# Neighbourhood attention with the value products of two heads side by side on column halves of the array, the bias row loaded ahead, and vector work spread over the feed-forward blocks

## The chip, the cores and the metric

One core of one Trainium2 chip runs the whole program. The metric is device time in microseconds (us), the median of the runs. Names of engines in the profile: PE is the matrix engine (TensorE), PEld its weight loads, DVE is VectorE, ACT is ScalarE, POOL is GpSimd, SP is SyncE, which issues nearly all DMAs.

## The reference, cut to what matters

Two blocks of two layers each work on 512 tokens of width 1024 (in the first block with 256 context tokens). Only three parts of the first block bear on the change: the neighbourhood attention of layer 0, the modulation vectors, and the feed-forward of both layers.

```
# layer 0: 16 heads of width 64, latent tokens on an 8 x 64 grid
s_loc = q_row . k_win + bias          # a window of 8 rows x 16 columns around each query
s_ctx = q_row . k_c                   # and all 256 context keys
p = softmax(concat(s_loc, s_ctx))
o = p[..., :n_loc] . v_win + p[..., n_loc:] . v_c
# context queries attend to the 256 context keys only; then out = o @ w_o
ada_mod = split(silu(cvec) @ ada_w[i] + ada_b[i], 6)      # shift, scale, gate vectors
ffn = (silu(h @ w_in_a) * (h @ w_in_u)) @ w_out
```

## The kernel before, in words

The program runs in phases: layer 0 mixer (to about 557 us), layer 0 feed-forward (to about 1190), layer 1 mixer, layer 1 feed-forward (1690 to 2075), then the second block. Weight products split both operands into a rounded high part and a rest and take three products (`mm3`, L146 to L148), each at one column a cycle.

**Attention (`na_heads`, L656 on).** A cell is one head `h` and one block `b` of 128 queries: 16 heads times 6 blocks (b 0 to 3 are latent and see 256 window keys and 256 context keys, b 4 and 5 are context and see 256). 96 cells run head by head, in a loop of steps `g`. Step `g` issues, in this order: the scores of cell g+1 (`na_scores`, PE, into `s`), the store of cell g-3 (`na_store`, DVE), the transposes of cell g-1's probabilities (`na_turn`, PE, `p` to `pt`), the maximum of cell g+1 (DVE), its exponential (ACT, which writes `p` and the sum into a column of `mx`), the value products of cell g-2 (`na_values`, PE), the copy of `pt` to `pT` (ACT for odd b, DVE for even b), and the reciprocal of the sum (`na_scale`, DVE). PE and DVE keep this order as written (`manual_schedule`); the other engines and the DMAs are put in order by the scheduler. Between these pieces `upto` issues units of the query, key and value projections (`pacc`, `ptq`), spread over the first 75 steps, and after them the units of `gemv_rows`. So the stage has a main stretch (about 75 to 412 us) and a tail (about 412 to 512 us) in which only the vector work is left to put between the cells.

The value product of a cell is `pT` (128 keys by 128 queries) as the stationary operand and 64 columns of `v` as the moving one, in plain float32: 4 products for a latent cell, 2 for a context cell, each of two instructions in the trace. The result has queries on partitions; `na_store` multiplies it by the reciprocal. `split_rows` (from step 84 on, one head pair each) transposes it with PE into `pacc` and splits it into `hT`, the operand of the output projection (`pw`).

**Modulation vectors.** `gemv_rows` (layer 0) works in 16 chunks of 256 columns: per chunk two `half` units load 512 KB (`araw`) and issue four products each on four column groups of 32 (`pg`, two result rows per group); ACT copies `pg` to `modx`, a DMA writes the bias row into row 2 of `modx`, and `total` (L475) adds the groups and the bias with one product. Five chunks run in the main stretch, eleven in the tail.
In the feed-forward blocks `gemv_jobs` computes 24 chunks for later layers on DVE (L430, L432: eight multiply-adds of 128x256 for each vector). After each of the 22 inner blocks `f`, `every` = 2 jobs are issued until none are left, so they sit behind f = 0 to 11; `gemv_flush` adds each result on PE behind the next block.

Of the kernel before, what the change touches and what calls it, by code (L numbers as in the profile page):

```python
# [9 lines left out]
F32 = mybir.dt.float32  # L10
# [5 lines left out]
OP = mybir.AluOpType  # L16
# [33 lines left out]
def fr(ap):  # L50
    return ap.bitcast(F32)
# [233 lines left out]
def ffn(S, l, xs, xout, more):  # L285
# [11 lines left out]
    fp, ps = S.tp, S.ps  # L297
    gts = []
    jobs = [j for wn, ll, p, vv in more for j in gemv_jobs(S, fp, wn, ll, p, vv, ps, ("gv", 1))]
    every = (len(jobs) + 18) // 19  # L300
    late = (1000, 300)[l]

    def dense(f):
# [19 lines left out]
    for gi, gn in enumerate(groups):  # L323
        gts = []
        for f in range(f0, f0 + gn):
            pa, pu, *pc = dense(f)
            out_mm = S.lastmm
            g = fp.tile([128, n], F32, name="g", tag="g", bufs=2)
            sa = fp.tile([128, n], F32, name="sa", tag="sa", bufs=2)
            nc.scalar.activation(sa[:, 0:512], pa, AF.Silu)  # L330
            if l == 0:
                gv = g[:, 0:512].rearrange("p (r c) -> p c r", r=ROWS)
                nc.vector.tensor_mul(gv, *[x.rearrange("p (c r) -> p c r", r=ROWS) for x in (sa[:, 0:512], pu)])
            else:
                nc.vector.tensor_mul(g[:, 0:512], sa[:, 0:512], pu)
            if nt == 6:
                nc.scalar.activation(sa[:, 512:768], pc[0][:, 0:256], AF.Silu)
                nc.vector.tensor_mul(g[:, 512:768], sa[:, 512:768], pc[0][:, 256:512])
            gh = fp.tile([128, n], F32R, name="gh", tag="gh", bufs=7)
            gl = fp.tile([128, n], F32R, name="gl", tag="gl", bufs=7)  # L340
            nc.scalar.activation(gh, g, AF.Copy)  # L341
            nc.vector.tensor_sub(gl, g, fr(gh))
            gts.append((gh, gl))
            gemv_flush(S, fp, ps, ("gv", 1), out_mm.ins)
            S.late = late
            for j in jobs[:every]:
                jobs.pop(0)()
        if ys is None:
            ys = [xout(t) for t in range(nt)]
            gates = [gate_bcast(S, "g2", l, v) for v in range(2 if nt == 6 else 1)]  # L350
        last = gi == len(groups) - 1
        Ws = []

        def out_tile(i, h):
            S.mark("ffn_out")
            p = ps.tile([128, 512], F32, name="po", tag="out", bufs=2)
            sl = slice(i * 128, (i + 1) * 128)
            for k in range(gn):
                S.mm3(p, [q[:, sl] for q in gts[k]], Ws[h](k), k == 0, k == gn - 1)
            residual_add(S, ys[i], p, gates[i // 4], h * 512, 512)  # L360

        cols = lambda h: S.weights([S.wcols(wo, h * 512, 512, f0, gn)], gn)
        if last:
            Ws += [cols(0), cols(1)]
            for i in range(nt):
                for h in range(2):
                    out_tile(i, h)
        else:
            for h in range(2):
                Ws.append(cols(h))  # L370
                for i in range(nt):
                    out_tile(i, h)
        f0 += gn
# [69 lines left out]
def gemv_rows(S, wname, layer, parts):  # L443

    nc, ps = S.nc, S.ps
    w = S.I[wname][layer]
    bias = S.I[{"ada_w": "ada_b", "w_ada_2": "b_ada_2"}[wname]]  # L450
    pg = ps.tile([128, 512], F32, name="pg", tag="gv", bufs=1)
    nc.vector.memset(pg[:, 0:256], 0.0)
    sel = S.sb.tile([128, 2], F32, name="sel4")
    nc.vector.tensor_reduce(sel, S.idf.rearrange("p (j v) -> p v j", j=4)[:, 0:2, :], axis=AX.X, op=OP.add)
    nc.vector.tensor_add(sel, sel, S.idf[:, 2:3].to_broadcast([128, 2]))
    todo = []

    def half(part, c, h):
        S.mark(f"gemv {part}{layer}")
        c0 = PARTS[wname].index(part) * D + c * 256  # L460
        raw = S.gvpool.tile([128, 4, 256], F32, name="araw", tag="araw", bufs=2)
        nc.sync.dma_start(raw, S.wcols(w, c0, 256, 4 * h, 4))
        for k in range(4):
            nc.tensor.matmul(pg[32 * k:32 * k + 2, 0:256], S.cc[:, 4 * h + k, :], raw[:, k, :], start=(h == 0),
                             stop=(h == 1))
        if h:
            x = S.gvpool.tile([128, 256], F32, name="modx", tag="modx", bufs=1)
            nc.scalar.activation(x, pg[:, 0:256], AF.Copy)
            nc.sync.dma_start(x[2:3, :], bias[layer:layer + 1, c0:c0 + 256])
            todo.append((part, c, x))  # L470

    def total():
        part, c, x = todo.pop(0)
        S.mark(f"gemv {part}{layer}")
        nc.tensor.matmul(pg[0:2, 256:512], sel, x, start=True, stop=True)  # L475
# [12 lines left out]
    out[-1].append((0.5, total))  # L488
    return out

# [167 lines left out]
def na_heads(S, na, hT, jobs):  # L658
# [11 lines left out]
    S.oT = oT = [S.x4(name="oT") for _ in range(6)]  # L670

    both = na.tile([128, 768], F32, name="bias")
    nc.gpsimd.memset(both[:, 256:512], 0.0)
    S.bias = [(both[:, o:o + 256], view(both, o, ([step, 2], [1, 256]))) for o, step in ((0, 256), (512, -256))]
    QK, V = {}, {}
# [30 lines left out]
            units.pop(0)[1]()  # L706


    cells = [(h, b) for h in range(16) for b in range(6)]
    st = {}  # L710
    fill(NA_HEAD)
    with S.tc.manual_schedule(engines=NA_ENG):
# [8 lines left out]
        for g in range(-1, 100):  # L721
# [3 lines left out]
            if cell(g + 1):  # L725
                h, b = cells[g + 1]
                assert S.nturn[h // 2] == 12, (g, h)
                if b == 0:
                    wide = na.tile([128, 384], F32, name="wide", tag="wide", bufs=2)
                    nc.sync.dma_start(wide, I["rpb_w"][h])  # L730
                    st["wide"] = wide
                st[g + 1] = {}
                na_scores(S, na, st, g + 1, h, b, QK[h // 2][h % 2], mask)
            if cell(g - 3):
                na_store(S, st.pop(g - 3), *cells[g - 3], oT)
            upto(g + NA_S[0])
            if cell(g - 1):
# [3 lines left out]
            upto(g + NA_S[1])  # L741
            if cell(g + 1):
                na_exp(S, st[g + 1], *cells[g + 1])
            if cell(g - 2):
                h = cells[g - 2][0]
                assert cells[g - 2][1] or len(V[h // 4][1]) == 3, g
                na_values(S, st[g - 2], *cells[g - 2], V[h // 4])
            if cell(g - 1):
                na_copy(S, st[g - 1], *cells[g - 1])
            if 84 <= g < 91:  # L750
# [183 lines left out]
                F.then(NA_LAGS[5] + NA_GAP * (2 * u + hh), lambda a=(tt, u, hh): turn(*a), 0.2)  # L934


def split_rows(S, oR, oT, pr):

    nc = S.nc
    S.mark("osplit")  # L940
    for ts, (hi, lo) in ((range(4), oR.row(pr)), (range(4, 6), oR.crow(pr))):
        pt = S.acc(128 * len(ts))
        for i, t in enumerate(ts):
            nc.tensor.transpose(pt[:, i * 128:(i + 1) * 128], oT[t][:, pr * 128:(pr + 1) * 128], S.idf)
        nc.scalar.activation(hi, pt, AF.Copy)
        nc.vector.tensor_sub(lo, pt, fr(hi))


def na_scores(S, na, st, g, h, b, qk, mask):
# [16 lines left out]
    me.update(s=s, p=S.t2("p", n), mx=sb.tile([128, 4], F32, name="mx", tag="mx", bufs=7))  # L966
    if lat:
        if b == 0 or BVAR[b] != BVAR[b - 1]:
            S.bias.reverse()
            o = BOFF[b] * 8  # L970
            nc.gpsimd.tensor_sub(S.bias[0][0], mask[:, BVAR[b], :], st["wide"][:, o:o + 256])
        me["bias"] = S.bias[0][1]


def na_max(S, me, h, b):
# [14 lines left out]

def na_scale(S, me):
    S.mark("attscale")
    r = me["mx"][:, 3:4]
    S.nc.vector.reciprocal(r, r)


def na_turn(S, me, h, b):
# [17 lines left out]
        nc.vector.tensor_copy(pT, pt)  # L1015


def na_values(S, me, h, b, V):
    nc = S.nc
    S.mark(f"att{h}.{b}")  # L1020
    vc = (h % 4) * 64
    vt, vs = V
    vv = vt[4:6]
    if b < 4:
        k0 = KBASE[b] * 8
        vv = [vt[k0 // 128 + j] if k0 % 128 == 0 else vs[k0 // 128 + j] for j in range(2)] + vv
    po = S.ps.tile([128, 64], F32, name="po", tag="pv", bufs=1)
    for j, v in enumerate(vv):
        nc.tensor.matmul(po, me["pT"][:, j, :], v[:, vc:vc + 64], start=(j == 0), stop=(j == len(vv) - 1))
    me["po"] = po  # L1030
# [754 lines left out]
```

## Time and profile before

| | us |
|---|---|
| median of 3 runs | 3476.13 (3475.0 to 3479.37) |
| the profiled execution: its own time | 3472.26 |
| its span, first to last instruction | 3470.5 |
| mean granted PE clock | 0.984 of full speed |

The profiled execution is the one from which every row below is taken. Its own time is 3.87 us under the median of the runs. PE is busy for 97% of the span, but a busy PE is not PE at its peak: the record of a short product lasts longer than the distance to the next one, so prices are read below from start to start.

### The profile page before, as it was taken

The page shows a single profiled execution, that of the slowest core. Times are in us where ns is not written, and L with a number is a line of the kernel's source. Part 1 is how long each engine was busy: PE and PEld are TensorE (multiplying, and loading weights), DVE is VectorE, ACT ScalarE, POOL GpSimd, SP SyncE. Part 2 cuts the span into 40 slices and gives each one's busy share as a digit, 9 for nine tenths or more (in the row PEclk, how much of TensorE's full clock was granted, in tenths as well). Part 3 has the DMA queues.
Part 4 walks back from the last instruction along what each step waited for, and adds up shares of the span by engine and source line. Part 5 has one row for each costly group of instructions (what it writes and reads, how often), then busy time and mean ns, then how long its engine had stood idle before and what let it go on. Part 6 is the DMA issues. An engine that isn't in the chain of part 4 may idle for free.

```text
span 3470.5 us, 49643 instructions
## 1 busy us (share of the span) xinstructions
PE 3355.7 (97%) x18924; PEld 2838.8 (82%) x18924; DVE 1892.7 (55%) x3745; ACT 1259.4 (36%) x2480; POOL 720.1 (21%) x650
## 2 busy tenths in 40 slices
PE   7999989999999999999999999999999999999999
PEld 5999857887788788888777878888888788888887
DVE  6456544649864556578778544435552334355523
ACT  4455533222222433334422334333333343333332
POOL 2122202111111211101322223121222221211222
PEclk9999989999999999999999999999999999999999
DMA  6122244324531121111556434232223432322333
GB/s 202 49 75 67 63 135 141 97 67 128 176 116 56 54 62 44 55 49 49 163 165 195 119 108 125 80 104 73 92 78 101 144 104 80 110 69 91 94 97 100
DMA packets 450206, 345.30 MB, mean 99 GB/s; under 512 B 40336, under 2 KB 421552, under 8 KB 449968
## 3 DMA queue, kind: packets, MB, share of 16 engines
q1 hardware_dynamic: 449536, 341.73, 32.9%
q8 instruction: 148, 2.42, 0.3%
q0 software_dynamic: 432, 0.41, 0.1%
q14 instruction: 90, 0.74, 0.1%
HBM read 328.34 MB, written 12.74 MB: 98 GB/s over the span
## 4 chain that ended last, share of the span: by engine, by line
PE 74%; DVE 7%; DMA 2%; ACT 2%; issue 1%; POOL 1%; DVEq 0%; SPq 0%; POOLq 0%; ACTq 0%
PE pacc L148 12%; PE pacc L147 12%; PE pacc L146 12%; PE pau L148 3%; PE pau L146 3%; PE pau L147 3%; PE po L146 3%; PE po L148 3%; PE po L147 3%; PE pw L148 2%; PE pw L146 2%; PE pw L147 2%; DVE gacc L432 2%; PE pl L1194 2%; DVE wlo L135 1%
## 5 line engine op out<-in xcount | busy, mean ns | idle before, releaser
L135 POOL TENSOR_TENSOR wlo<-wraw,whi 128x512 fp32r<-128x512 f32 x388 | 526.7, 1359 | 2121.9 <-ACT whi L132 1762.1
L132 ACT ACTIVATE whi<-wraw 128x512 fp32r<-128x512 f32 x776 | 485.2, 631 | 796.9 <-PE pacc L147 357.8
L135 DVE TENSOR_TENSOR wlo<-wraw,whi 128x512 fp32r<-128x512 f32 x388 | 332.1, 857 | 552.1 <-ACT whi L132 547.4
L148 PE MATMUL pacc<-hT,wlo 128*128 128x512 f32 x1344 | 535.1, 398 | 0.0
L146 PE MATMUL pacc<-hT,whi 128*128 128x512 f32 x1344 | 534.6, 398 | 0.0
L147 PE MATMUL pacc<-hT,whi 128*128 128x512 f32 x1344 | 532.0, 396 | 0.0
L146 PE MATMUL pacc<-whi,hT 128*128 128x256 f32 x1056 | 307.4, 291 | 5.0 <-DVE h L607 2.9
L148 PEld LDWEIGHTS pacc<-hT,wlo 128*128 128x128 f32 x1344 | 252.8, 188 | 58.3
L147 PEld LDWEIGHTS pacc<-hT,whi 128*128 128x128 f32 x1344 | 252.7, 188 | 57.7
L147 PE MATMUL pacc<-wlo,hT 128*128 128x256 f32 x1056 | 299.4, 284 | 0.2 <-DVE wlo L813 0.2
L148 PE MATMUL pacc<-whi,hT 128*128 128x256 f32 x1056 | 298.4, 283 | 0.0
L146 PEld LDWEIGHTS pacc<-hT,whi 128*128 128x128 f32 x1344 | 253.0, 188 | 54.7
L146 PE MATMUL pau<-hT,whi 128*128 128x512 f32 x704 | 280.0, 398 | 0.7 <-DVE h L607 0.7
L148 PE MATMUL pau<-hT,wlo 128*128 128x512 f32 x704 | 280.2, 398 | 0.0
L147 PE MATMUL pau<-hT,whi 128*128 128x512 f32 x704 | 279.1, 396 | 0.0
L432 DVE SCALAR_TENSOR_TENSOR gacc<-araw,cact,gacc 128x256 f32<-128x256 f32 x392 | 222.0, 566 | 23.8 <-DMA araw<-ada_w 10.6
L146 PEld LDWEIGHTS pacc<-whi,hT 128*128 128x128 f32 x1056 | 200.5, 190 | 7.7 <-DVE h L607 3.1
L147 PEld LDWEIGHTS pacc<-wlo,hT 128*128 128x128 f32 x1056 | 200.9, 190 | 2.0 <-DVE wlo L813 0.4
L148 PEld LDWEIGHTS pacc<-whi,hT 128*128 128x128 f32 x1056 | 200.4, 190 | 0.0
L146 PE MATMUL po<-whi,gh 128*128 128x512 f32 x440 | 177.7, 405 | 17.0 <-ACT gh L341 15.7
L147 PE MATMUL po<-wlo,gh 128*128 128x512 f32 x440 | 175.6, 400 | 0.0
L148 PE MATMUL po<-whi,gl 128*128 128x512 f32 x440 | 175.1, 400 | 0.1
(375 smaller groups left out, 6600.4 us busy)
## 6 DMA issues: line engine op xcount, KB each, us to landing
araw<-ada_w SPq DMA_DIRECT2D x96, 512.0 KB
wraw<-w_in SPq DMA_DIRECT2D x96, 512.0 KB
wraw<-ffn_w_in SPq DMA_DIRECT2D x176, 256.0 KB
wraw<-w_in SPq DMA_DIRECT2D x160, 256.0 KB
araw<-w_ada SPq DMA_DIRECT2D x48, 512.0 KB
wraw<-ffn_w_out SPq DMA_DIRECT2D x40, 512.0 KB
x<-x SPq DMA_DIRECT2D x24, 512.0 KB
wraw<-hg_w_in SPq DMA_DIRECT2D x24, 512.0 KB
```

The lines of the kernel that those rows point to most:

```text
L132: nc.scalar.activation(hi, r, AF.Copy)
L135: eng.tensor_sub(lo, r, fr(hi))
L146: nc.tensor.matmul(out, lh[0], rh[0], start=first, stop=False)
L147: nc.tensor.matmul(out, lh[0], rh[1], start=False, stop=False)
L148: self.lastmm = nc.tensor.matmul(out, lh[1], rh[0], start=False, stop=last)
L432: nc.vector.scalar_tensor_tensor(acc, r, cv, acc, op0=OP.mult, op1=OP.add)
L1194: nc.tensor.matmul(pl[:, c, :], KX[:, c * 128:(c + 1) * 128], view(Q, c * 128, ([2 * m, 64 // m], [LAT + m, 2], [1, m])), start=True, stop ...
```

## The change

It does four things.
1. **Value products.** The 96 cells run in pairs of heads: (2p, b), (2p+1, b). In every odd step the products of both cells of a pair are issued together: now 64 columns of `v` are stationary and `pT` moves (128 columns), the first head goes to output partitions 0 to 63 and the second to 64 to 127, that is to one half of the array's columns each. The result has the head's channels on partitions, so the four transposes in `split_rows` are gone, and one copy per pair replaces two stores. As queries no longer stand on partitions there, DVE scales `p` by the reciprocal before the transposes (`na_scale`). The bias tiles belong to the parity of the head, and the `wide` tiles of a pair are loaded at its start.
2. **Bias row apart.** Its DMA goes to row 98 of `modx`, which ACT doesn't write, and is issued at the chunk's first half instead of behind the ACT copy.
3. **Vectors spread.** The 24 jobs of a feed-forward block go to f = 0 to 19 in proportion: two behind f = 0, 5, 10 and 15, one behind each other one.
4. **By itself**: `split_rows` no longer takes two `pacc` banks, which the output projection uses.

```diff
@@ ffn
-    every = (len(jobs) + 18) // 19
+    njobs = len(jobs)
-            for j in jobs[:every]:
+            while jobs and (njobs - len(jobs)) * 20 < njobs * (f + 1):
                 jobs.pop(0)()
@@ gemv_rows
+    m = 3 * 32 + 2
+        if h == 0:
+            x = S.gvpool.tile([128, 256], F32, name="modx", tag="modx", bufs=1)
+            nc.sync.dma_start(x[m:m + 1, :], bias[layer:layer + 1, c0:c0 + 256])
+            todo.append((part, c, x))
         if h:
-            x = S.gvpool.tile([128, 256], F32, name="modx", tag="modx", bufs=1)
-            nc.scalar.activation(x, pg[:, 0:256], AF.Copy)
-            nc.sync.dma_start(x[2:3, :], bias[layer:layer + 1, c0:c0 + 256])
-            todo.append((part, c, x))
+            nc.scalar.activation(todo[0][2][0:m, :], pg[0:m, 0:256], AF.Copy)
@@ na_heads
-    cells = [(h, b) for h in range(16) for b in range(6)]
+    cells = [(2 * pr + i, b) for pr in range(8) for b in range(6) for i in range(2)]
-            if cell(g - 3):
+            if cell(g - 3) and g % 2 == 0:
-            if cell(g - 2):
+            if cell(g - 2) and g % 2:
-                na_values(S, st[g - 2], *cells[g - 2], V[h // 4])
+                na_values(S, [st[g - 3], st[g - 2]], *cells[g - 2], V[h // 4])
@@ split_rows
-        pt = S.acc(128 * len(ts))
-        for i, t in enumerate(ts):
-            nc.tensor.transpose(pt[:, i * 128:(i + 1) * 128], oT[t][:, pr * 128:(pr + 1) * 128], S.idf)
-        nc.scalar.activation(hi, pt, AF.Copy)
-        nc.vector.tensor_sub(lo, pt, fr(hi))
+        nc.scalar.activation(hi, o_row(oT, pr, lat), AF.Copy)
+        nc.vector.tensor_sub(lo, o_row(oT, pr, lat), fr(hi))
@@ na_scale
     S.nc.vector.reciprocal(r, r)
+    S.nc.vector.tensor_scalar(p, p, r, None, op0=OP.mult)
@@ na_values
-    po = S.ps.tile([128, 64], F32, name="po", tag="pv", bufs=1)
+    po = S.ps.tile([128, 128], F32, name="po", tag="pv", bufs=1)
     for j, v in enumerate(vv):
-        nc.tensor.matmul(po, me["pT"][:, j, :], v[:, vc:vc + 64], start=(j == 0), stop=(j == len(vv) - 1))
+        for i, me in enumerate(two):
+            nc.tensor.matmul(po[64 * i:64 * i + 64, :], v[:, vc + 64 * i:vc + 64 * i + 64], me["pT"][:, j, :],
+                             start=(j == 0), stop=(j == len(vv) - 1))
@@ na_store
-    S.nc.vector.tensor_scalar(oT[b][:, h * 64:(h + 1) * 64], me["po"], me["mx"][:, 3:4], None, op0=OP.mult)
+    S.nc.vector.tensor_copy(o_row(oT, h // 2, b < 4)[:, (b % 4) * 128:(b % 4 + 1) * 128], me["po"])
```

The new line numbers are some lines higher. Three places show how the order moves.

DVE in the main stretch, before: one step and the start of the next (`s,mx` is the maximum, `cat` and `qn` belong to the projections).

```order
L1015 COPY pT<-pt 128x256
L994 RECIPROCAL mx<-mx 128x1
L1036 TENSOR_SCALAR oT<-po,mx 128x64
L477 COPY modb<-pg 2x256
L884 TENSOR_TENSOR qn<-pacc,gain 128x2x128 x2
L981 ISA s,mx<-s,bias 128x512
```

The same place after the change: the scaling of `p` follows each reciprocal, and the store is a copy that comes once in two steps.

```order
L1023 COPY pT<-pt 128x512
L1001 RECIPROCAL mx<-mx 128x1
L1002 TENSOR_SCALAR p<-p,mx 128x512
L1046 COPY oT<-po 128x128
L479 COPY modb<-pg 2x256
L887 TENSOR_TENSOR qn<-pacc,gain 128x2x128 x2
L988 ISA s,mx<-s,bias 128x512
```

What moved: one operation more per step between a cell's sum and whatever DVE does next, and half a store less.

PE in the tail, before: one chunk of the vector work between the cells (L944 are the transposes of `split_rows`).

```order
L1029 MATMUL po<-vs,pT 128x64 x2
L1029 MATMUL po<-v,pT 128x64 x2
L944 MATMUL pacc<-idf,oT 128x128 x6
L475 MATMUL pg<-modx,sel_477 2x256
L964 MATMUL s<-qk 128x256 x2
L464 MATMUL pg<-araw,cc 2x256 x4
L1003 MATMUL pt<-idf,p 128x128 x4
```

After: the transposes are gone, and products of the output projection (`pw`) stand between the cells; 46 of them come before the last value product, where there were 13.

```order
L1039 MATMUL po<-pT,v 64x128 x8
L477 MATMUL pg<-modx,sel_477 2x256
L971 MATMUL s<-qk 128x512 x2
L146 MATMUL pw<-whi,hT 128x512
L147 MATMUL pw<-wlo,hT 128x512
L148 MATMUL pw<-whi,hT 128x512
```

SP in the tail, before: the bias row `modx` is issued behind or between the `araw` loads that come after its chunk.

```order
L478 DMA row_sc_0_482<-modb 2x256
L462 DMA araw<-ada_w 128x4x256 x2
L469 DMA modx<-ada_b 1x256
L478 DMA row_sc_0_482<-modb 2x256
```

After: it is issued ahead of the two `araw` loads of the next chunk.

```order
L464 DMA modx<-ada_b 1x256
L480 DMA row_sc_0_482<-modb 2x256
L467 DMA araw<-ada_w 128x4x256 x2
L464 DMA modx<-ada_b 1x256
```

What moved: the row's DMA now waits for the `total` of the chunk before (one buffer) instead of for this chunk's ACT copy.

## Rows read from the trace of the kernel before

**Rows 1.** Windows: us, busy time (instructions) per engine, PEclk, DMA share, GB/s.
```profile
174.00:412.00 238.00, 236.86 (x2003) 223.58 (x2003) 140.91 (x396) 125.06 (x327) 55.64 (x61) 1.00 0.23 68
412.00:512.00 100.00, 81.24 (x548) 51.38 (x547) 43.14 (x130) 37.58 (x100) 11.15 (x13) 0.81 0.41 119
```
**Rows 2.** Waits of PE, 412 to 516 us: total, times, longest.
```profile
PE pg L475 <- DMA modx<-ada_b: 13.0, 8, 3.4
```
**Rows 3.** Timeline of PE, main stretch: start, us, engine, line, operation, count.
```profile
200.59 0.62 PE L1003 MATMUL pt<-idf,p 128*128 128x128 f32 x4
200.97 0.36 PE L146 MATMUL pacc<-whi,hT 128*128 128x256 f32 x1
...
205.75 1.00 PE L1029 MATMUL po<-v,pT 128*128 128x64 f32 x8
206.56 0.36 PE L146 MATMUL pacc<-whi,hT 128*128 128x256 f32 x1
206.76 0.28 PE L147 MATMUL pacc<-wlo,hT 128*128 128x256 f32 x1
206.88 0.29 PE L148 MATMUL pacc<-whi,hT 128*128 128x256 f32 x1
...
210.44 0.55 PE L1029 MATMUL po<-v,pT 128*128 128x64 f32 x4
210.80 0.43 PE L922 MATMUL ptq<-idr,cat 128*128 128x128 f32 x3
```
**Rows 4.** Timeline of PE around one half of a chunk (four column groups).
```profile
184.68 0.38 PE L1003 MATMUL pt<-idf,p 128*128 128x128 f32 x2
185.00 0.61 PE L464 MATMUL pg<-araw,cc 128*2 128x256 f32 x8
185.54 0.66 PE L1029 MATMUL po<-v,pT 128*128 128x64 f32 x4
186.01 0.42 PE L922 MATMUL ptq<-idr,cat 128*128 128x128 f32 x3
```
**Rows 5.** Timeline of PE, second block: 128 moving columns, whole array.
```profile
2192.98 1.16 PE L1520 MATMUL o<-PT,V 128*128 128x128 f32 x8
2193.97 0.60 PE L1506 MATMUL pt<-idf,P 128*128 128x128 f32 x4
```
**Rows 6.** Groups by line and shape, DVE: count | busy us, mean ns | idle before, releaser.
```profile
L1036 DVE TENSOR_SCALAR oT<-po,mx 128x64 f32<-128x64 f32 x96 | 26.3, 274 | 35.2 <-PE po L1029 34.7
L1504 DVE TENSOR_SCALAR P<-P,bM 128x256 f32<-128x256 f32 x56 | 17.6, 386 | 0.0
L1173 DVE TENSOR_SCALAR ks<-K,omlb 128x512 f32<-128x512 f32 x8 | 3.8, 481 | 19.3 <-ACT K L1165 19.3
L1234 DVE COPY s<-pk 128x128 f32<-128x128 f32 x16 | 4.6, 288 | 4.4 <-PE pk L1231 4.3
```
**Rows 7.** Timeline of PE where the output projection begins.
```profile
513.37 0.39 PE L148 MATMUL pw<-whi,hT 128*128 128x512 f32 x1
513.60 0.39 PE L146 MATMUL pw<-whi,hT 128*128 128x512 f32 x1
```
**Rows 8.** Waits of PE in the two feed-forward blocks (700 to 1000; 1690 to 2075 us).
```profile
PE po L146 <- ACT gh L341: 7.0, 3, 5.8
PE pg L508 <- ACT gacc L434: 4.8, 4, 2.3
PE po L146 <- ACT gh L341: 7.1, 2, 4.5
```
**Rows 9.** Windows in the two feed-forward blocks, columns as in rows 1.
```profile
880.00:920.00 40.00, 34.20 (x157) 27.48 (x155) 36.36 (x66) 7.78 (x15) 5.38 (x4) 0.91 0.59 176
...
1770.00:1810.00 40.00, 35.47 (x154) 28.27 (x153) 32.09 (x61) 12.80 (x24) 8.08 (x6) 0.95 0.75 222
```
**Rows 10.** Timeline of DVE ahead of PE's wait of 5.8 us at 886 us.
```profile
885.46 2.05 DVE L432 SCALAR_TENSOR_TENSOR gacc<-araw,cact,gacc 128x256 f32<-128x256 f32 x4 [0.47 <-DMA araw<-ada_w]
```
**Rows 11.** Windows in the tail, columns as in rows 1.
```profile
424.00:448.00 24.00, 22.77 (x104) 13.00 (x104) 7.39 (x23) 5.87 (x16) 1.34 (x2) 0.50 0.35 113
```

More of the change, by code (lines that the diff above doesn't have):

```diff
@@ L453, in gemv_rows @@
     sel = S.sb.tile([128, 2], F32, name="sel4")
+    m = 3 * 32 + 2
     nc.vector.tensor_reduce(sel, S.idf.rearrange("p (j v) -> p v j", j=4)[:, 0:2, :], axis=AX.X, op=OP.add)
-    nc.vector.tensor_add(sel, sel, S.idf[:, 2:3].to_broadcast([128, 2]))
+    nc.vector.tensor_add(sel, sel, S.idf[:, m:m + 1].to_broadcast([128, 2]))
     todo = []
@@ L474, in total @@
         S.mark(f"gemv {part}{layer}")
-        nc.tensor.matmul(pg[0:2, 256:512], sel, x, start=True, stop=True)
+        nc.tensor.matmul(pg[0:2, 256:512], sel[0:m + 1, :], x[0:m + 1, :], start=True, stop=True)
         b = S.t2("modb", 256)[0:2, :]
@@ L672, in na_heads @@
     both = na.tile([128, 768], F32, name="bias")
+    S.wide = {}
     nc.gpsimd.memset(both[:, 256:512], 0.0)
@@ L728, in na_heads @@
                 if b == 0:
-                    wide = na.tile([128, 384], F32, name="wide", tag="wide", bufs=2)
-                    nc.sync.dma_start(wide, I["rpb_w"][h])
-                    st["wide"] = wide
+                    S.wide[h] = na.tile([128, 384], F32, name="wide", tag="wide", bufs=2)
+                    nc.sync.dma_start(S.wide[h], I["rpb_w"][h])
                 st[g + 1] = {}
                 na_scores(S, na, st, g + 1, h, b, QK[h // 2][h % 2], mask)
-            if cell(g - 3):
+            if cell(g - 3) and g % 2 == 0:
+                st.pop(g - 4)
                 na_store(S, st.pop(g - 3), *cells[g - 3], oT)
@@ L934, in qk_feed, with o_row @@
                 F.then(NA_LAGS[5] + NA_GAP * (2 * u + hh), lambda a=(tt, u, hh): turn(*a), 0.2)
+def o_row(oT, pr, lat):
+    if lat:
+        return oT[pr // 2][:, (pr % 2) * 512:(pr % 2 + 1) * 512]
+    return oT[4 + pr // 4][:, (pr % 4) * 256:(pr % 4 + 1) * 256]
 def split_rows(S, oR, oT, pr):
@@ L940, in split_rows @@
     S.mark("osplit")
-    for ts, (hi, lo) in ((range(4), oR.row(pr)), (range(4, 6), oR.crow(pr))):
-        pt = S.acc(128 * len(ts))
-        for i, t in enumerate(ts):
-            nc.tensor.transpose(pt[:, i * 128:(i + 1) * 128], oT[t][:, pr * 128:(pr + 1) * 128], S.idf)
-        nc.scalar.activation(hi, pt, AF.Copy)
-        nc.vector.tensor_sub(lo, pt, fr(hi))
+    for lat, (hi, lo) in ((True, oR.row(pr)), (False, oR.crow(pr))):
+        nc.scalar.activation(hi, o_row(oT, pr, lat), AF.Copy)
+        nc.vector.tensor_sub(lo, o_row(oT, pr, lat), fr(hi))
 def na_scores(S, na, st, g, h, b, qk, mask):
@@ L965, in na_scores @@
     me = st[g]
-    me.update(s=s, p=S.t2("p", n), mx=sb.tile([128, 4], F32, name="mx", tag="mx", bufs=7))
+    me.update(s=s, p=S.t2("p", n), mx=sb.tile([128, 4], F32, name="mx", tag="mx", bufs=4))
     if lat:
+        bias = S.bias[h % 2]
         if b == 0 or BVAR[b] != BVAR[b - 1]:
-            S.bias.reverse()
             o = BOFF[b] * 8
-            nc.gpsimd.tensor_sub(S.bias[0][0], mask[:, BVAR[b], :], st["wide"][:, o:o + 256])
-        me["bias"] = S.bias[0][1]
+            nc.gpsimd.tensor_sub(bias[0], mask[:, BVAR[b], :], S.wide[h][:, o:o + 256])
+        me["bias"] = bias[1]
 def na_max(S, me, h, b):
@@ L992, in na_scale @@
     S.mark("attscale")
-    r = me["mx"][:, 3:4]
+    p, r = me["p"], me["mx"][:, 3:4]
     S.nc.vector.reciprocal(r, r)
+    S.nc.vector.tensor_scalar(p, p, r, None, op0=OP.mult)
 def na_turn(S, me, h, b):
@@ L1015, in na_copy, with na_values @@
         nc.vector.tensor_copy(pT, pt)
-def na_values(S, me, h, b, V):
+def na_values(S, two, h, b, V):
     nc = S.nc
     S.mark(f"att{h}.{b}")
-    vc = (h % 4) * 64
+    vc = (h % 4 - 1) * 64
     vt, vs = V
@@ L1026, in na_values @@
         vv = [vt[k0 // 128 + j] if k0 % 128 == 0 else vs[k0 // 128 + j] for j in range(2)] + vv
-    po = S.ps.tile([128, 64], F32, name="po", tag="pv", bufs=1)
+    po = S.ps.tile([128, 128], F32, name="po", tag="pv", bufs=1)
     for j, v in enumerate(vv):
-        nc.tensor.matmul(po, me["pT"][:, j, :], v[:, vc:vc + 64], start=(j == 0), stop=(j == len(vv) - 1))
-    me["po"] = po
+        for i, me in enumerate(two):
+            nc.tensor.matmul(po[64 * i:64 * i + 64, :], v[:, vc + 64 * i:vc + 64 * i + 64], me["pT"][:, j, :],
+                             start=(j == 0), stop=(j == len(vv) - 1))
+    two[1]["po"] = po
 def na_store(S, me, h, b, oT):
     S.mark(f"att{h}.{b}")
-    S.nc.vector.tensor_scalar(oT[b][:, h * 64:(h + 1) * 64], me["po"], me["mx"][:, 3:4], None, op0=OP.mult)
+    S.nc.vector.tensor_copy(o_row(oT, h // 2, b < 4)[:, (b % 4) * 128:(b % 4 + 1) * 128], me["po"])
 LEVELS = (1, 2, 4, 8, 16, 32, 64)
```

## The prediction

> **What bounds the kernel now.** I read the table of engines first (PE 97% of the span), then the windows of the attention stage, then the list of PE's waits there, and last the timeline of PE at the pieces that the diff touches. From 174 to 412 us PE has work for 236.86 of 238 us at full clock, while DVE has work for 140.91, which is 59% [rows 1]. So in the main stretch a microsecond less of PE instructions is a microsecond less of time, and DVE has room. In the tail (412 to 512 us) PE has work for 81 of 100 us at a mean clock of 0.81 [rows 1]. Its largest wait there is for the bias row: 13.0 us in 8 waits [rows 2]. In the feed-forward blocks PE waits little, 7.0 and 4.8 us in layer 0 and 7.1 us in layer 1 [rows 8], but the clock is also down around these waits: 0.91 and 0.95 in the windows that hold them [rows 9].
>
> **Value products.** Before, a latent cell is eight instructions from 205.75 to 206.56, 0.81 us, and the product behind it takes 0.20 us to the next start where its successor takes 0.12 [rows 3]; I count this 0.08 with the cell: 0.89. A context cell is 210.44 to 210.80, 0.36, and with the same 0.08 it is 0.44 [rows 3]. There are 32 latent pairs and 16 context pairs, so the values cost 32 x 1.78 + 16 x 0.88 = 71 us now.
>
> After, a latent pair is 16 instructions of 128 columns, eight on each half. Nothing in the trace runs two halves, but the vector products run four column groups: eight instructions of 256 columns take 185.00 to 185.54, 0.54 us [rows 4]. Behind them a four-instruction value product takes 186.01 - 185.54 = 0.47, which is 0.11 over its 0.36, so coming back costs 0.11. Ahead of them two transposes take 0.32 [rows 4], where four take 0.38 in the main stretch, 0.095 each [rows 3]; so going in costs about 0.13. Inside, the eight instructions are two rounds of four at once: (0.54 - 0.11)/2 = 0.215 us for 256 columns, so 0.107 for 128. One after the other they would be eight times that. The groups therefore run together, and I take the halves to do the same, as their rows are the nearest: 8 rounds x 0.107 + 0.25 for going in and out = 1.11 us per latent pair, 0.43 + 0.25 = 0.68 per context pair. That saves 0.67 x 32 + 0.20 x 16 = **25 us**.
>
> The bounds of this term come from the case that they don't run together. 128 moving columns on the whole array cost (2193.97 - 2192.98)/8 = 0.124 us per instruction [rows 5]. 640 instructions (32 x 16 + 16 x 8) one after the other are then 79 us, with 48 x 0.25 = 12 for the mode 91 us: 20 us more than now, not 25 less. If the weight loads were not hidden either, it would be worse (rivals).
>
> **Transposes of split_rows.** 48 go. Four take 0.38 us at 200.59 [rows 3]: 48 x 0.095 = **4.6 us** less on PE, full clock.
>
> **DVE.** Per latent pair it gains two scalings of 128x512 (a like one: 0.481) and one copy (0.288), and loses two stores (0.274 each) [rows 6]: +0.70. Per context pair, with 0.386 for 256 columns, it is +0.51. Together 32 x 0.70 + 16 x 0.51 = 30.6 us more on DVE, which takes its share in the main stretch from 59% to about 66%. PE's work covers it: a cell's sum is there at the end of step g and its transposes come in step g+2, about a whole step (some 4 us) later. What queues behind the scaling is the next maximum, on which the exponential waits, one step ahead of need as well. Without that cover the whole 30 us would be on the path. I charge **+3** for single late steps (0 to +22).
>
> **Bias row.** In the tail the 13.0 us [rows 2] are waits of `total` for a small DMA issued behind the ACT copy, in SP's queue between 512 KB loads. Now the row is loaded a half ahead, so `total` waits for the ACT copy instead. `total` stands right behind value products or behind `pw` products, and a chunk still needs two `araw` loads, the copy and the sum in turn. What is late next is `araw`. Also `modx` has one buffer, so SP, with the row at its head, holds the next `araw` loads until the `total` before is through. I take **-10** (0 to -14).
>
> **Output projection earlier.** With no `pacc` bank taken by `split_rows`, 46 rather than 13 `pw` products stand before the last value product; each is 513.60 - 513.37 = 0.23 us [rows 7], 33 x 0.23 = 7.6 us of work that comes into a tail that has 19 us of idle time. The bias row already takes most of that, so I count half: **-4** (0 to -8).
>
> **Vectors spread.** Behind each of f = 0 to 11 DVE has two jobs. Its chain of multiply-adds waits for an `araw` load at 885.46 [rows 10], `g` and `gh` for the feed-forward queue behind it, and PE then waits 5.8 us for `gh` [rows 8]. The waits are 7.0 + 4.8 + 7.1 = 18.9 us [rows 8], and the loss of clock in these two windows, (0.09 + 0.05) x 40 us = 5.6 [rows 9], is with their neighbours some 7. One job per block needs 512 KB less in the same time, so I let two thirds of 26 go, 17. At the end of each block three jobs now stand later than before, and their sums come close to the next phase: I add 3 back. **-14** (0 to -24).
>
> **Not counted.** From 424 to 448 us PE runs at a clock of 0.50 with 22.77 of 24 us busy [rows 11], behind a gap in the tail; at full clock half of that, 11 us, would be saved. Whether the gap stays, the rows can't say: a bound of -11. The `wide` tiles, now loaded for both heads of a pair at once, come later relative to need; the bound is a few us at seven pair changes. The copies in ACT's place in `split_rows` are the same work from another source.
>
> **Sum.** -25 - 4.6 + 3 - 10 - 4 - 14 = -54.6. The profiled execution took 3472.3, so 3417.7; it lies 3.9 under the median of the runs, to which I forecast: **3422**.
>
> **Rivals.**
> (1) *The halves run one after the other*, so that the change does not do what it says. Values cost 20 more instead of 25 less: 3422 + 45 = **3467**, by little still faster. Against it stand the four groups in rows 4. For it: those have a stationary operand of 2 columns, these 64. 7%.
> (2) *Weight loads stand between the products* (the other side). PE's loads in the main stretch are 223.58 us for 2003, 0.112 each [rows 1]; a load of half the columns is at a proportional estimate 0.056. If each of the 640 instructions waits for its own load and runs alone, it costs 0.107 + 0.056 = 0.163: 104 + 12 = 116 us against 71, so +45, and 3422 + 70 = **3492**. It decides from 0.139 us per instruction (640 x 0.139 + 12 = 71 + the 30 saved elsewhere). Against it: on the whole array load and product together come every 0.124 [rows 5], so most of a load is hidden there. 6%. The Trainium skill, "TensorE: Matmul & The Clock Gate", Part 3, The mechanism, says that a weight load overlaps running products only where its row group differs, and the halves share all rows; this rule speaks against the change, and rows 4 can't refute it, since their loads are of two columns. By another of its pages, "TensorEngine Tiling (Array Packing)", Key Properties, different tiles load weights and multiply in parallel, which would leave the 3422; no row here has halves, so none decides between the two.
> (3) *DVE comes onto the path*: an average share of 66% hides steps in which a cell's copy, scaling, maximum and projection work meet. Then most of the 30 us is paid, +25 for +3: **3444**. For it: DVE's part of a step is in one order with nothing to overtake. 13%.
> (4) *The feed-forward waits only move*, to the sums at the blocks' ends or to `araw`, which limits both ways: no gain there, 3422 + 14 = **3436**. 15%.
> (5) *The tail keeps its clock*: the gap before 424 closes, another -11: **3411**. 15%.
>
> **How the numbers follow.** The forecast has 44%; its own range is 3410 to 3433. For 8 in 10 the range takes rivals 3 to 5 with the forecast's own spread and leaves out 1, 2 and a few in 100 at the lower end: 3394 (the lower bounds of bias row, vectors and clock together: -4 - 10 - 11, and the 3 of DVE) to 3458 (rival 3 and rival 4 together). A difference within 0.2%, 7 us, can't be told from none in this kernel: that is 3469 to 3483. Rivals 1 (half of it) and 2 (a little) touch it: same 0.04. Slower: rival 2 and what is left of mishaps not listed, 0.07. Faster: 0.89.
>
> **What would show it.** Right: a latent pair takes 1.0 to 1.2 us from its first value product to the next line, and PE stays above 98% busy up to the tail; the wait of `total` for a DMA is gone from the list of waits and nothing over 4 us stands in its place; the stage ends some 40 us earlier; the waits for `gh` fall under 5 us and the clock in both windows of rows 9 is 0.97 or more. Wrong: a pair of 2 us or more (rivals 1, 2), a new wait of the transposes for DVE's scaled `p` or of the scores for the maximum (3), new waits for `gacc` or `modrow` near 1190 and 2075 us (4). A transfer that is late at the head of SP's queue would upset the tail's terms, 14 of the 55 us.

## The result, and the profile after

The changed kernel takes 3434.51 us (median of 4 runs, 3432.11 to 3435.18) against 3475.57 us for the kernel before (median of 4 runs): a ratio of 0.9879, 95% interval 0.9862 to 0.9896. That is 41 us less, inside the stated range (3394 to 3458), where about 54 were forecast (3422). The profiled execution has a span of 3430.3 us, 40.2 less than before.

The first thing to read is where each phase begins in the two traces. Timeline of PE before, at the start of the first feed-forward (`pau`), of the transposes and products that open layer 1 (`pt`, `pv`), of the second feed-forward and of the second block:

```profile
590.55 0.51 PE L146 MATMUL pau<-hT,whi 128*128 128x512 f32 x1 [0.67 <-DVE h L607]
...
1186.31 1.91 PE L598 MATMUL pt<-idf,xn 128*128 128x128 f32 x16
1193.29 1.01 PE L146 MATMUL pv<-whi,hT 128*128 128x256 f32 x3
...
1685.94 0.79 PE L146 MATMUL pau<-hT,whi 128*128 128x512 f32 x1
2075.97 1.27 PE L598 MATMUL pt<-idf,xn 128*128 128x128 f32 x9
```

The same places after (1135.18 is the end of the feed-forward's products, as 1186.31 is before):

```profile
548.87 0.50 PE L146 MATMUL pau<-hT,whi 128*128 128x512 f32 x1 [0.67 <-DVE h L609]
...
1135.18 0.40 PE L510 MATMUL pg<-gacc,ones 128*128 128x256 f32 x2
1136.44 0.50 PE L510 MATMUL pg<-gacc,ones 128*128 128x256 f32 x2 [0.86 <-DVE modrow L511]
1138.60 0.47 PE L510 MATMUL pg<-gacc,ones 128*128 128x256 f32 x2 [1.66 <-DVE modrow L511]
1143.46 1.11 PE L600 MATMUL pt<-idf,xn 128*128 128x128 f32 x4 [4.38 <-ACT xn L586]
...
1158.69 1.22 PE L146 MATMUL pv<-whi,hT 128*128 128x256 f32 x4
...
1650.80 0.80 PE L146 MATMUL pau<-hT,whi 128*128 128x512 f32 x1
2033.63 1.47 PE L600 MATMUL pt<-idf,xn 128*128 128x128 f32 x12
```

From these rows: the attention stage ends 41.7 us earlier (590.55 to 548.87; the forecast's terms for it add up to 40.6). The first feed-forward takes 586.3 instead of 595.8, 9.5 us less. The way from its end to the first `pv` takes 23.5 instead of 7.0, 16.5 us more. The second feed-forward takes 382.8 instead of 390.0, 7.2 us less. The second block, which the diff does not touch, begins 42.3 us earlier and ends only 40.2 us earlier; where those 2.1 us go is open. So the attention gave what was forecast, the blocks with the spread vectors gained 16.7 us, and 16.5 were lost again at one place.

Windows of the main stretch after, which answers to [rows 1] (it now ends some 10 us earlier), and of the tail up to the last value product, which stands at 519 us before (second window) and at 485 us after (third window):

```profile
174.00:402.00 228.00, 224.72 (x2004) 202.97 (x2002) 157.36 (x424) 128.75 (x337) 55.66 (x62) 1.00 0.24 71
```

```profile
412.00:519.00 107.00, 88.24 (x591) 56.65 (x591) 44.70 (x136) 39.42 (x105) 11.15 (x13) 0.82 0.42 121
```

```profile
412.00:485.00 73.00, 67.16 (x522) 36.02 (x524) 44.78 (x128) 28.78 (x77) 6.38 (x9) 0.92 0.66 187
```

DVE's share in the main stretch rose from 59% to 69%, and PE is busy for 98.6% of it (99.5% before). In the tail PE now has work for 92% of the time where it had 82%, and the clock is 0.92 where it was 0.82. The waits of PE in the tail after (412 to 516 us), against [rows 2]:

```profile
PE pg L469 <- DMA araw<-ada_w: 4.6, 8, 1.2
PE ptq L925 <- DVE cat L915: 2.3, 1, 2.3
PE pg L477 <- ACT modx L472: 0.3, 1, 0.3
PE pt L1011 <- DVE p L1002: 0.2, 1, 0.2
```

The wait for the bias row is gone; `total` waits 0.3 us for the ACT copy. `araw` comes next with 4.6 us in eight waits, none over 1.2 us; by the prediction's sign nothing over 4 us was to stand in the row's place, so this sign was just missed. The new values, timeline of PE after (rows against [rows 3]):

```profile
251.63 0.66 PE L1039 MATMUL po<-pT,v 128*64 128x128 f32 x8
252.22 0.39 PE L146 MATMUL pacc<-whi,hT 128*128 128x256 f32 x1
252.44 0.28 PE L147 MATMUL pacc<-wlo,hT 128*128 128x256 f32 x1
...
266.35 0.28 PE L148 MATMUL pacc<-whi,hC 128*128 128x256 f32 x1
266.56 1.09 PE L1039 MATMUL po<-pT,v 128*64 128x128 f32 x16
267.58 0.45 PE L925 MATMUL ptq<-idr,cat 128*128 128x128 f32 x3
```

A latent pair takes 267.58 - 266.56 = 1.02 us from start to start, a context pair 252.22 - 251.63 = 0.59. Before it went 1.62 (two times 0.81) and 0.72.

### The profile page after: what moved, and what is told of

Its sections match the earlier page's. It is cut to its first block, busy times and chain, and to the rows that moved or that the text cites. A ratio compares the mean times of both kernels' runs of the same rounds, so it can differ in the third digit from the quotient of the medians.

```text
span 3430.3 us, 49594 instructions
## 1 busy us (share of the span) xinstructions
PE 3317.5 (97%) x18876; PEld 2791.9 (81%) x18876; DVE 1925.0 (56%) x3807; ACT 1257.9 (37%) x2480; POOL 722.6 (21%) x650
## 4 chain that ended last, share of the span: by engine, by line
PE 82%; DVE 8%; DMA 4%; ACT 3%; issue 2%; POOL 1%; SPq 0%; DVEq 0%; POOLq 0%; ACTq 0%
PE pacc L146 14%; PE pacc L147 14%; PE pacc L148 14%; PE pau L148 3%; PE pau L146 3%; PE pau L147 3%; PE po L146 3%; PE po L148 3%; PE po L147 2%; DVE gacc L432 2%; PE pw L148 2%; PE pw L146 2%; DMA araw<-ada_w 2%; PE pw L147 2%; PE pl L1204 2%
```

## The experiments

Ten kernels were run. The times beside them are medians; the effects of parts are also read from the start of the first feed-forward in each profile. The changed kernel was timed in a set of runs of its own, and the median of the kernel before lies between 3475.57 and 3478.65 us in the four sets, so a difference of 3 us from the change can't be told from none.

**The spread vectors: is the loss at the entrance of layer 1 theirs?** Timeline of ACT after, around the wait (ACT squares `x` into `xn` at L168; the last column says what the idle time ended on):

```profile
1123.86 0.62 ACT L168 ACTIVATE xn<-x 128x512 f32<-128x512 f32 x1
...
1142.07 0.63 ACT L168 ACTIVATE xn<-x 128x512 f32<-128x512 f32 x1 [17.50 <-DMA row_g<-modrow]
```

The norm of layer 1 squares its first block of 128 tokens by 1124.4 us; the second waits 17.5 us for the DMA that writes out the last modulation row. It does not read that row, a gate's. But `modrow`, `modb` and `gacc2` lie in the feed-forward's pool, and the `xn` tiles belong to the next pool, which takes over memory of the one before. So the wait is read here as one for memory. Before, the same squares ran between the last products, held only by `x` itself. ACT before, the second block of tokens, 17 us ahead of the end of the products (1186.31):

```profile
1169.06 0.63 ACT L168 ACTIVATE xn<-x 128x512 f32<-128x512 f32 x1 [1.34 <-DVE x L540]
```

DVE after shows the chain that ends there, three sums whose `modb` and `modrow` have one buffer each:

```profile
1135.99 0.40 DVE L511 TENSOR_TENSOR modrow<-modb,pg 1x256 f32<-1x256 f32 x1
...
1138.05 0.41 DVE L511 TENSOR_TENSOR modrow<-modb,pg 1x256 f32<-1x256 f32 x1 [1.06 <-DMA modb<-ada_b]
1140.49 0.41 DVE L511 TENSOR_TENSOR modrow<-modb,pg 1x256 f32<-1x256 f32 x1 [2.04 <-DMA modb<-ada_b]
```

Four kernels test this. The first has the old placing of the jobs:

```diff
-            while jobs and (njobs - len(jobs)) * 20 < njobs * (f + 1):
+            for j in jobs[:2]:
                 jobs.pop(0)()
```

> The changed kernel with the vector jobs placed as before (two behind each of f = 0 to 11); value pairs and bias row stay. Theory: the spread gains some 9.5 us in the blocks of layer 0 and 7 in those of layer 1, and gives about 16 back at the entrance of layer 1, where the norm waits for the row of the last sums; so it is worth nothing in sum and this kernel takes 3431 to 3438 us, with the waits for gh and gacc back and the entrance of layer 1 short (7 us from the first transpose to the first pv product). Rival (the gains in the blocks are not the spread's, the entrance is): about 3420. Rival (the spread is worth the 14 us of the forecast): 3449.

Measured: 3437.42 us (3436.24 to 3438.04), within the range expected, and 2.9 above the change. The waits in the blocks of layer 0 are back, and the entrance of layer 1 is short again (7.0 us from the end of the products to `pv`). PE's waits in these blocks:

```profile
PE po L146 <- ACT gh L341: 9.1, 6, 6.3
PE pg L510 <- ACT gacc L434: 5.9, 4, 3.0
```

So the spread as it stands is worth about 3 us or nothing, not 14: by the ratios to the kernel before in their own runs the two kernels are 0.9885 and 0.9879, each within 0.0017. The second kernel spreads layer 1 alone:

```diff
-            while jobs and (njobs - len(jobs)) * 20 < njobs * (f + 1):
+            while jobs and (njobs - len(jobs)) * (12, 20)[l] < njobs * (f + 1):
```

> The changed kernel with the jobs of layer 0 placed as before and those of layer 1 spread over f = 0 to 19. Theory: layer 1 keeps its gain of 7 us and the entrance of layer 1 has no wait: 7 us less than with the old placing in both layers, 3426 to 3431 us. Rival (the spread's gain in layer 1 is given back later too): as with the old placing, 3431 to 3438.

Measured: 3426.53 us (3425.36 to 3429.08), 10.9 under the old placing in the same set of runs, at the edge of what was expected: layer 1 keeps its gain. By the profiles 7.9 us of it lie in the second feed-forward. The third spreads layer 0 over 16 blocks, so that its sums end before the last products do:

```diff
-            while jobs and (njobs - len(jobs)) * 20 < njobs * (f + 1):
+            while jobs and (njobs - len(jobs)) * (16, 20)[l] < njobs * (f + 1):
```

> The changed kernel with the jobs of layer 0 spread over f = 0 to 15 (three behind every second block, one behind the others) and those of layer 1 as in the change. By the order the last sum of layer 0 then stands about 100 products (24 us) ahead of the end of the feed-forward. Theory: the wait at the entrance of layer 1 goes (13 to 16 us), and of the 9.5 us of the blocks most stays: 3417 to 3424 us. Rival (three jobs in a block bring the waits for gh back): 3426 to 3430.

Measured: 3417.54 us (3416.69 to 3420.63), ratio to before 0.983 (0.9815 to 0.9845): 17 us less than the change and the best of all kernels here (19.9 less than the old placing in the same set of runs). Its entrance to layer 1, timeline of PE; ACT's second block of tokens there; and PE's wait for `gh` in the blocks of layer 0:

```profile
1139.32 1.91 PE L600 MATMUL pt<-idf,xn 128*128 128x128 f32 x16
...
1146.30 0.73 PE L146 MATMUL pv<-whi,hT 128*128 128x256 f32 x4 [0.42 <-ACT whi L132]
```

```profile
1122.15 0.63 ACT L168 ACTIVATE xn<-x 128x512 f32<-128x512 f32 x1 [1.33 <-DVE x L542]
```

```profile
PE po L146 <- ACT gh L341: 3.3, 6, 0.6
```

The entrance is back at 7.0 us as before the change, the squares run between the products again, and PE's waits for `gh` stay short (longest 0.6 us). The expectation misreads its own edit: 24 jobs over 16 blocks are two behind every second block and one behind the others, nowhere three, so the rival of three jobs in a block was not tried. The profile is 15.0 us shorter than the change's: 16.5 less at the entrance, but 4.7 more in the blocks of layer 0. The fourth leaves the spread as it is and gives the buffers of the sums a pool of their own (in layer 1 too):

```diff
-    with S.psum() as S.ps, S.tc.tile_pool(name="ffn", bufs=1, reuse_waits="tile") as S.tp:
+    with S.psum() as S.ps, S.tc.tile_pool(name="rowp", bufs=1, reuse_waits="tile") as S.rp, \
+            S.tc.tile_pool(name="ffn", bufs=1, reuse_waits="tile") as S.tp:
...
-            a2 = pool.tile([128, 2, 256], F32R, name="gacc2", tag="gacc2", bufs=4)
+            a2 = S.rp.tile([128, 2, 256], F32R, name="gacc2", tag="gacc2", bufs=4)
...
-            b, r = [pool.tile([1, 512], F32, name=x, tag=x, bufs=1) for x in ("modb", "modrow")]
+            b, r = [S.rp.tile([1, 512], F32, name=x, tag=x, bufs=1) for x in ("modb", "modrow")]
```

> The changed kernel with the buffers of the sums (gacc2, modb, modrow) in a pool of their own beside the feed-forward's, so that the norm of layer 1 writes into memory that the late sums don't hold; the jobs stay spread as in the change. Theory (the norm waits for memory, not for the work): ACT's wait of 17.5 us and PE's 13 us for xn at the entrance of layer 1 go, and 3420 to 3425 us. Rival (the late sums themselves hold up the norm, by DVE's and PE's order): no change, 3432 to 3436.

Measured: 3426.68 us (3422.73 to 3429.17), 7.8 less than the change, between the theory's range and the rival's. ACT no longer waits for the row. ACT's first square, and PE from the end of the products to `pv`:

```profile
1137.63 0.63 ACT L168 ACTIVATE xn<-x 128x512 f32<-128x512 f32 x1 [12.10 <-PE po L148]
```

```profile
1137.44 0.40 PE L512 MATMUL pg<-gacc,ones 128*128 128x256 f32 x2
...
1156.39 0.74 PE L146 MATMUL pv<-whi,hT 128*128 128x256 f32 x4
```

The squares start while the three sums are still running, so the late sums as work were not what held the norm; in the change it was the buffers they held. But ACT still starts only behind the last output products, 12.1 us idle, where before the squares ran between them, and the entrance still takes 19.0 us (1137.44 to 1156.39) instead of 23.5. What it waits for there was not tried; moving the buffers also moved every other tile of the pool. So this kernel, read by its profile (the slowest of its four runs), takes away the wait for the row and with it 4.6 of the 16.5 us; the kernel with 16 blocks takes away all 16.5 by ending the jobs earlier. What holds the norm for the other 12 us once the row doesn't is open.

**The halves of the array.** The order within a pair decides whether neighbours are on different halves:

```diff
-    for j, v in enumerate(vv):
-        for i, me in enumerate(two):
+    for i, me in enumerate(two):
+        for j, v in enumerate(vv):
```

> The changed kernel with the value products of a pair in another order: all of the first head, then all of the second, so that neighbours are on the same half of the columns. Theory (halves run together only when neighbours are on different halves, and loads are hidden): 16 x 0.107 + 0.25 = 1.96 us for a latent pair, 1.11 for a context pair, against 1.1 and 0.7, which is 34 us more, in the tail partly absorbed: 3460 to 3470 us. Rival (a later product on the other half may start ahead of those before it, so the order doesn't matter): 3434. Rival (loads of one half are not hidden when neighbours share it, 0.163 each): latent pair 2.9 us, 3490 to 3505.

Measured: 3444.56 us (3443.11 to 3447.4), 10 more than the change; the first feed-forward starts 13 us later (561.84 against 548.87). Both my expectation (+26 or more) and the first rival (0) missed. Timeline of PE of this kernel, a latent and a context pair:

```profile
249.70 1.58 PE L1039 MATMUL po<-pT,v 128*64 128x128 f32 x16
251.21 0.39 PE L146 MATMUL pacc<-whi,hC 128*128 128x256 f32 x1
...
257.55 0.67 PE L1039 MATMUL po<-pT,v 128*64 128x128 f32 x8
258.14 0.39 PE L146 MATMUL pacc<-whi,hT 128*128 128x256 f32 x1
```

The latent pair costs 1.51 us instead of 1.02, the context pair 0.59 as ever. The single starts in the trace explain it: of the eight instructions on the first half four start alone; the second half's first starts at 250.19, 6 ns behind the fifth and ahead of the last three; four of each run side by side; then the last four of the second half run alone, 0.109 us apart. In the context pair, with four on each half, the second half starts 13 ns behind the first. So an instruction started ahead of three earlier ones on the other half, but not of more. That makes twelve rounds where the change has eight: 4 x 0.109 = 0.44 of the 0.49 us. Over 32 pairs 0.49 us is 15.7, of which the stage shows 13. One half working alone also takes 0.109 each with its own weight load, which settles the price of the loads.

**The bias row.** In the change, with the row put back behind the ACT copy:

```diff
-        if h == 0:
-            x = S.gvpool.tile([128, 256], F32, name="modx", tag="modx", bufs=1)
-            nc.sync.dma_start(x[m:m + 1, :], bias[layer:layer + 1, c0:c0 + 256])
-            todo.append((part, c, x))
...
         if h:
-            nc.scalar.activation(todo[0][2][0:m, :], pg[0:m, 0:256], AF.Copy)
+            x = S.gvpool.tile([128, 256], F32, name="modx", tag="modx", bufs=1)
+            nc.scalar.activation(x, pg[:, 0:256], AF.Copy)
+            nc.sync.dma_start(x[2:3, :], bias[layer:layer + 1, c0:c0 + 256])
+            todo.append((part, c, x))
```

> The changed kernel with the bias row loaded as before, behind the ACT copy, into row 2 of modx. Theory (the row's wait was worth 10 us in the tail, as forecast): 3441 to 3447 us, with total waiting for the row's DMA again, 10 us or more in sum. Rival (the output products that now stand in the tail hide the row): 3433 to 3437.

Measured: 3458.83 us (3457.46 to 3460.69), 24.3 more than the change, about twice the top of what I expected (6.5 to 12.5 more). And the other way round, the kernel before with the row alone (the same lines, + and - exchanged):

> The kernel before with the bias row alone loaded ahead as in the change. Theory: the 13.0 us of waits for the row go and 10 to 13 us of the time with them, in the tail: 3463 to 3467 us. Rival (the next wait, for araw, takes their place): 3473 to 3477. If the clock then also stays up in the tail, under 3460.

Measured: 3458.88 us (3456.62 to 3460.99), 17.8 less than the kernel before in the same runs (3476.7). That is more than the 10 to 13 expected and agrees with the expectation's last sentence, on the clock. Third, the kernel before with the value pairs and what goes with them, but the old row and the old placing:

> The kernel before with the value pairs and what belongs to them (scaling of p, no transposes in split_rows), but with the old bias row and the old placing of the vector jobs. Theory (in the tail the row's wait takes what the pairs save; only the main stretch and the tail's last part gain): 15 to 17 us less than before, 3457 to 3462 us, with over 20 us of waits for the row. Rival (the forecast's terms for values, transposes, scaling and output products hold without the row): 30 us less, 3443 to 3448.

Measured: 3461.93 us (3461.23 to 3464.32), 13.9 less than before in its runs (3475.78), in the range expected. First feed-forward in the three kernels (old row, row only, pairs only), each from its own timeline:

```profile
574.73 0.50 PE L146 MATMUL pau<-hT,whi 128*128 128x512 f32 x1 [0.66 <-DVE h L607]
```

```profile
570.72 0.51 PE L146 MATMUL pau<-hT,whi 128*128 128x512 f32 x1 [0.66 <-DVE h L609]
```

```profile
572.89 0.50 PE L146 MATMUL pau<-hT,whi 128*128 128x512 f32 x1 [0.66 <-DVE h L607]
```

From 590.55, the row alone brings the stage 19.8 us and the pairs alone 17.7; in the change the row is worth 25.9 (574.73 to 548.87) and the pairs 21.9 (570.72 to 548.87). PE's waits in the tail with the old row, in the changed kernel and with the pairs only:

```profile
PE pg L475 <- DMA modx<-ada_b: 22.1, 8, 5.2
```

```profile
PE pg L475 <- DMA modx<-ada_b: 21.8, 8, 3.9
```

The same eight waits were 13.0 us before [rows 2]. Where the pairs made the other work of the tail shorter, the wait for the row grew by 9 us. Windows from 412 us to the last value product, PEclk third from the end, of the change with the old row and of the kernel before with the new one:

```profile
412.00:513.00 101.00, 78.24 (x533) 42.92 (x534) 45.00 (x128) 27.82 (x75) 7.09 (x9) 0.83 0.49 140
```

```profile
412.00:498.00 86.00, 77.76 (x587) 51.10 (x585) 43.87 (x136) 39.67 (x105) 11.08 (x13) 0.92 0.54 151
```

The clock follows the row, with the value pairs and without them: 0.83 with its waits and 0.92 without in the changed kernel, 0.82 and 0.92 in the kernel before. An estimate from these windows: the clock took (1 - 0.82) x 107 = 19 us of the old tail and (1 - 0.92) x 86 = 7 of the tail with the row ahead, 12 less. With the 13.0 us of waits that is somewhat more than the 19.8 that the stage gained.

**The scaling on DVE.** Left out here: `p` is not multiplied by the reciprocal, so the output is not normalised.

```diff
     S.nc.vector.reciprocal(r, r)
-    S.nc.vector.tensor_scalar(p, p, r, None, op0=OP.mult)
```

> The changed kernel without the scaling of p by the reciprocal on DVE (the probabilities are left unnormalised), 37 us less work on DVE. Theory (PE's work hides it but for single late steps): 2 to 4 us less, 3430 to 3433 us. Rival (DVE is on the path in each step): 15 us less or more, under 3420.

Measured: 3428.12 us (3427.86 to 3429.37), 6.4 less than the change, a little more than the 2 to 4 expected. But the attention stage, the only place of the edit, ends at the same time:

```profile
548.74 0.50 PE L146 MATMUL pau<-hT,whi 128*128 128x512 f32 x1 [0.66 <-DVE h L609]
```

That is 0.13 us earlier, with 43 us less on DVE (the two groups below). So the scaling is hidden altogether, and rival 3 is out. The two profiles differ by 4.1 us, all but 0.1 of it in phases that the edit does not touch, 2.1 of it in the second block; why is open. Groups of DVE after, by line and shape:

```profile
L1002 DVE TENSOR_SCALAR p<-p,mx 128x512 f32<-128x512 f32 x64 | 32.1, 501 | 2.2
...
L1046 DVE COPY oT<-po 128x128 f32<-128x128 f32 x48 | 13.7, 286 | 13.6 <-PE po L1039 13.3
...
L1002 DVE TENSOR_SCALAR p<-p,mx 128x256 f32<-128x256 f32 x32 | 11.3, 354 | 1.1
```

**The kernel before with the better spread alone** (jobs over 16 blocks in layer 0 and 20 in layer 1, the lines of the third kernel above):

> The kernel before with only the vector jobs spread, over f = 0 to 15 in layer 0 and f = 0 to 19 in layer 1. Theory (the spread gains in the blocks of both layers alike, whatever the attention does, and with 16 gives nothing back): 16 to 20 us less than before, 3456 to 3461 us. Rival (the gain depends on the earlier start of the blocks): 3468 or more.

Measured: 3461.16 us (3455.83 to 3461.22), 14.6 less than before (3475.78), ratio 0.9958 (0.9943 to 0.9972). That is a little under the 16 to 20 expected, and well below the rival's 3468: the gain does not need the earlier start.

## Why the prediction was right, and which steps were not

The measured 3434.5 us lie in the stated range, but just above the forecast's own range (3410 to 3433) and next to rival 4 (3436). The halves do run together, which decided between faster and slower; several of the terms were off, and some of them cancelled.

**Values: right in mechanism, a little too high in price.** The halves run together: 1.02 and 0.59 us per pair, eight or four rounds of 0.109. Going in and coming out cost more than the 0.25 counted: products that otherwise follow at 0.12 take 0.21 to the pair (266.35 to 266.56) and 0.22 behind it (252.22 to 252.44), so 0.19 comes on top of the bare 1.02 and 0.59. A latent pair is then 1.21 (1.11 forecast) and a context pair 0.78 (0.68), and the term is 32 x 0.57 + 16 x 0.10 = 20 us rather than 25. Rivals 1 and 2 are out: sixteen instructions one after the other would take 1.7 us at 0.107, more with a load between them, and the sixteen of a latent pair take 1.02. By the Trainium skill, "TensorE: Matmul & The Clock Gate", Part 3, The mechanism, a weight load overlaps running products only where its row group differs; here the trace differs from it. PE's loads of this line take 139 ns each by the record (count, busy us, mean ns):

```profile
L1039 PEld LDWEIGHTS po<-pT,v 128*64 128x64 f32 x512 | 28.8, 139 | 6.5 <-issue 2.4 <-PE pt L1011 0.9 <-ACT woh L132 0.4
```

Eight of them on one half would be 1.1 us by themselves, and the whole pair with its eight products per half takes 1.02. One half alone also starts an instruction with its own load every 0.109 us (the kernel with the other order). The halves share all rows, so loads do overlap products without a difference in rows. The trace agrees with the Trainium skill, "TensorEngine Tiling (Array Packing)", Key Properties, by which different tiles load and multiply in parallel.

**DVE: right in size, and its scaling free.** The added work is 32.1 + 11.3 + 13.7 - 26.3 (the old stores, [rows 6]) = 30.8 us against the 30.6 worked out. The charge of 3 us for late steps was not the scaling's: without it the stage ends where it did.

**Bias row: about half of what it was worth.** The term was 10 us with a bound of 14, and the runs show 18 to 24. I took the 13.0 us of recorded waits as a ceiling less something. Two things make it more. The recorded wait is what is left after other work has covered part of it, and the change itself took cover away: 22.1 us without the new row. And the waits pull the clock down, which I had put under "not counted" and rival 5: up to the last value product the clock is 0.92 rather than 0.82, and the windows of the two kernels with the row exchanged show that it goes with the row. Rival 5 came true in part (a stretch at 0.50 is left, 412 to 420 us); it did not lower the time below the forecast because the other terms fell short.

**Values in the tail, transposes and output projection: not worth their sum alone.** The forecast gave value pairs, transposes, scaling and output products 31 us together; alone they gave the stage 17.7, since in the tail the wait for the row took what they saved. With the row out of the way they gave 21.9. The rest of the sum of 40.6 came from the row. So the total for the stage was met to 1 us by two errors of opposite sign: that is luck, and I would have been wrong on either edit alone.

**Vectors spread: right in the blocks, wrong at their end.** The blocks gave 9.5 + 7.2 = 16.7 us where 17 were forecast. That is no sharper than some 4 us: the blocks of layer 0 take 586.3 us in the change and 590.3 in the kernel with buffers of their own, which has the same placing, and against the old placing in the changed kernel the gains are 13.3 and 8.7. The waits for `gh` fell, in layer 0 from 8.6 us over the whole feed-forward (7.0 of them in [rows 8]) to 2.8, in layer 1 from 7.1 to 3.2, and `gacc` is gone from the list. The clock is 1.00 in the windows that lie where those of [rows 9] did:

```profile
838.00:878.00 40.00, 40.00 (x177) 32.07 (x176) 36.62 (x64) 7.34 (x13) 5.72 (x4) 1.00 0.47 136
1735.00:1775.00 40.00, 40.00 (x175) 32.28 (x174) 29.49 (x55) 12.62 (x22) 7.85 (x6) 1.00 0.69 211
```

The step that failed is "I add 3 back": it was 16.5. I had counted the three late sums as work in the way. What the runs show instead is that ACT could not square `x` between the last products: in the change it waited 17.5 us for a buffer of the sums, and ending the jobs four blocks earlier takes the whole 16.5 away, while buffers of their own take away 4.6. The 13.5 us more than counted are as large as the gap between 3422 and 3434.5, and rival 4 (the waits move to the sums at the blocks' ends, 3436) describes what came.

## What to carry to other kernels

A job that is put off to the end of a phase keeps its buffers to the end of the phase, and a tile of the next phase can wait for them even when it needs nothing of the job: spread work so that it ends some blocks early (in layer 0, 16 of 22 blocks took 17 us less than 20 did). A wait in a list is what is left after other work has hidden part of it, so removing the work that hides it makes the wait grow; two edits to one stage must be priced together. Before a sum that comes out right is believed, its terms want separate runs.

## What was not expected of the hardware

Products on the two halves of the columns overlap although they are issued in one order: with four on one half and then four on the other they still ran side by side in full, with eight and eight four of each did. Two halves of 64 columns with their own loads run at 0.109 us per round, for each half what a half by itself takes. The tail's low clock [rows 11] needed no work taken out of PE to rise: with the row's waits alone gone the tail runs at 0.92 where it ran at 0.82.
